# A 31-tap depthwise convolution in a shared PSUM bank: prompt and sample instructions declared independent

## The chip, the cores and the metric

One core of one Trainium2 chip runs the whole program in one launch. The metric is device microseconds (us) of one execution, the median of the runs shown. The engines are named as in the profile: PE is TensorE's matrix multiplication and PEld its weight load, DVE is VectorE, ACT ScalarE, POOL GpSimd, SP SyncE.

## What is computed

One layer of a hybrid decoder for a prompt (16 learned meta tokens and 256 new tokens, 272 columns) and for 8 running sequences with 8 new tokens each (64 columns). A combined input projection feeds a Conformer convolution module and a Mamba-2 (SSD) mixer; an output projection and a layer of product-key experts (PEER) follow. The part that is changed is the depthwise convolution of the Conformer module: each of 1024 channels is filtered along time with 31 taps, over the 30 rows before the new ones (zeros for the prompt, a cache for the sequences) and the new rows.

```python
glu_in, z, xbc, dt_raw, gate_raw = jnp.split(xn @ w_in + b_in, ...)
u = ga * jax.nn.sigmoid(gb)                               # the two halves of glu_in
conf_cat = jnp.concatenate([conf_buf, u], axis=1)         # 30 rows of history, then the new rows
c = causal_depthwise(conf_cat, conf_dw_w, conf_dw_b)      # 31 taps, one filter for each channel
c = jax.nn.silu(layernorm(c, conf_ln_g, conf_ln_b))
y_a = c @ w_conf_out + b_conf_out
...
y = y @ w_m_out                                           # of the SSD mixer
x = x + (g_a * y_a + g_b * y_b) @ w_o
x = x + peer(rmsnorm(x, norm2_w), peer_w_q, peer_keys, peer_u, peer_v)
```

## The kernel before

Features lie on the 128 partitions and tokens in the free dimension: T = 336 columns, first the 64 sample columns (S0 = 64), then the 272 prompt columns (TP). The 1024 channels of the convolution are 8 blocks of 128.

The first stage is a loop over 8 head groups g. For each group it projects four blocks for the SSD mixer (`xbc`, with the short 4-tap convolution `conv_short`, L400 on DVE), two blocks for the gate z (`zproj`), then the two blocks of the Conformer module for the next group (`glu(g+1)`, whose product is written by L459 and L460) and its long convolution (`conf(g+1)` calls `conv_long`), then the decay tables (`decays`), then the SSD step itself (`ssd(g)`). `conf(0)` runs ahead of the loop. After the loop come the layer norm of the convolution's output, the remaining gates, the output projections (to about 620 us) and the expert layer, whose two streams of weights (`eraw`) fill the time from about 700 us to the end.

`conv_long` keeps the running sum of a block in one PSUM tile `pcv` (128 x 336 f32, one bank, one buffer with the tag `pb`). The first tap is a ScalarE activation (L388), the other 30 are `scalar_tensor_tensor` instructions on VectorE (L390): sum = input x tap weight + sum. Each tap is two instructions, one for the 272 prompt columns and one for the 64 sample columns, because the input columns of the sequences are strided. The last tap writes to `cbuf` in SBUF. So a block has 60 instructions on VectorE, and all eight blocks 480.

Within `ssd(g)` VectorE does, among other things: `bst` (L519) and `wsl` (L523), the low parts of split operands; `cbm` (L514), a masked product out of PSUM; `dec` (L516), the decay table times `cbm`; `hs` (L542, L545), the state; `yo` and `xg` (L570, L568), the output; `st` (L584), the new state. TensorE's products `pcb`, `pst`, `pq`, the transposes `ptr` and `pgn` share two PSUM buffers (tag `misc`); `pj` has three.

The order of the instructions on each engine is not written out by hand. The Tile framework draws a dependency between any two instructions that touch the same PSUM bank of a tile when at least one writes, and between those that touch the same data; it plans each engine's order at build time by simulating the program, with the order of the source as priority, and turns each dependency into a semaphore wait. Two VectorE instructions on different columns of `pcv` therefore depend on each other, and each instruction of a block waits for the one before it. The order of ScalarE's table-bound activations is chained by hand (`chain`), and TensorE's order is pinned to the source in the last group (`pin`).

Of the kernel before, what the change touches and what calls it, by code (L numbers as in the profile page):

```python
# [13 lines left out]
OP = mybir.AluOpType  # L14
# [120 lines left out]
def body(tc, ia, oa, stop=None):  # L135
    nc = tc.nc
    with ExitStack() as top:
# [40 lines left out]
        def V(name, j):  # L178
            o, n = VEC[name]
            return vec[:, o + j:o + j + 1]  # L180
# [193 lines left out]
        def samp(ap):  # L374
            return ap.rearrange("p (q c) -> p q c", q=NQ)

        def conv_long(cat, j, dst):
            cs = samp(cat[:, CC + TP:])
            acc = ps.tile([128, T], F32, name="pcv", tag="pb", bufs=1)
            for w in range(CW):  # L380
                wv = V("conf_w", j * CW + w)
                to = dst if w == CW - 1 else acc
                for lo, hi, i_ in ((S0, T, cat[:, w:w + TP]), (0, S0, cs[:, :, w:w + TS])):
                    a_, o = acc[:, lo:hi], to[:, lo:hi]
                    if lo == 0:
                        a_, o = samp(a_), samp(o)
                    if w == 0:
                        nc.scalar.activation(o, i_, AF.Identity, scale=wv, bias=V("conf_b", j))  # L388
                    else:
                        nc.vector.scalar_tensor_tensor(o, i_, wv, a_, op0=OP.mult, op1=OP.add)  # L390

        def conv_short(cat, j, dst, of):
            n = MCAT - MC
# [281 lines left out]
        def conf(g):  # L675
            conv_long(glu(g), g, cb[:, g, :])
            if 0 < g < G - 1:
                nc.gpsimd.tensor_tensor(csum, csum, cb[:, g, :], op=OP.add)
            elif g == 0:
                nc.gpsimd.tensor_copy(csum, cb[:, g, :])  # L680
# [74 lines left out]
        for j in range(KD):  # L755
# [8 lines left out]
                                           op0=OP.mult, op1=OP.subtract)  # L764
# [55 lines left out]
        for k in range(KD):  # L820
            nc.vector.scalar_tensor_tensor(nd[:, k, :], xT[:, k, NGAT:NGAT + ND], V("n2", k), rs2[:, NGAT:NGAT + ND],
                                           op0=OP.mult, op1=OP.mult)
# [521 lines left out]
```

## Time and profile before

| | |
|---|---|
| median of 3 runs | 1453.44 us (1450.84 to 1455.16) |
| the profiled execution | 1455.07 us |
| span in its profile | 1453.3 us, 24685 instructions |
| mean granted TensorE clock | 0.968 |
| busy: PE, DVE, POOL, ACT | 1348.9, 1070.6, 617.2, 527.0 us |

The profiled execution took 1.6 us more than the median; 1.8 us of it lie outside the span. Times in the views count from the span's start. A row of a timeline has the start, the duration, the engine, the source line, the operation, what it writes and reads, the shapes, and a count; neighbours of one kind are merged into one row, whose duration reaches from the first start to the last end, and a row that begins with a prompt instruction (128x272) can hold sample instructions (128x64) too. In brackets stands the idle time of the engine before the row and what ended it. A row of the waits has the total, the number of waits and the longest.

### The profile page before, as it was taken

How to read it: one execution, taken by the hardware profiler on the slowest of the kernel's cores; microseconds unless marked ns; L12 is line 12 of the kernel's file. 1: busy time of each engine (PE TensorE's matmuls, PEld its weight loads, DVE VectorE, ACT ScalarE, POOL GpSimd, SP SyncE). 2: the span in 40 equal slices, each digit the busy share in tenths (PEclk: the TensorE clock that was granted, in tenths of full speed). 3: DMA queues.
4: the chain of work that ended last, by engine and by line, in shares of the span. 5: the costliest groups of instructions: out<-in, count | busy, mean ns of one | idle time of the engine just before them, and what ended most of it. 6: DMA issues, size and time to landing. Idle time of an engine off the chain costs nothing.

```text
span 1453.3 us, 24685 instructions
## 1 busy us (share of the span) xinstructions
PE 1348.9 (93%) x9308; PEld 1276.7 (88%) x9308; DVE 1070.6 (74%) x2343; ACT 527.0 (36%) x1426; POOL 617.2 (42%) x491
## 2 busy tenths in 40 slices
PE   6999988999978999999999988999979999987997
PEld 3888987889857999989899888999979999987997
DVE  6788888888897522568999985877888777776423
ACT  4687657775737443434222221211111101011001
POOL 2267776676755665754221242222332222242200
PEclk9899999999989999999999999999989999999999
DMA  5434434444323344453999899999999999999983
GB/s 196 148 102 164 165 117 136 149 155 161 107 77 102 117 145 145 137 189 102 354 414 413 332 412 415 397 376 391 407 398 415 381 377 371 382 416 416 414 325 95
DMA packets 86807, 382.06 MB, mean 263 GB/s; under 512 B 10112, under 2 KB 15360, under 8 KB 66080
## 3 DMA queue, kind: packets, MB, share of 16 engines
q1 hardware_dynamic: 64144, 226.87, 43.6%
q0 software_dynamic: 20736, 151.00, 25.7%
q10 hardware_dynamic: 1808, 2.61, 0.5%
q8 instruction: 73, 1.20, 0.3%
q14 instruction: 46, 0.38, 0.1%
HBM read 367.41 MB, written 13.03 MB: 262 GB/s over the span
## 4 chain that ended last, share of the span: by engine, by line
PE 66%; DVE 18%; DMA 8%; ACT 6%; issue 1%; POOL 0%; DVEq 0%; ACTq 0%
PE pj L149 25%; PE va L1210 19%; PE pj L1119 11%; PE pg L1148 4%; DMA eraw<-in_vE_dram 3%; DMA eraw<-in_uT_dram 3%; DVE pcv L390 2%; DVE ygat L1053 2%; DVE wuv L1045 2%; PE pst L149 2%; ACT wh L213 1%; ACT dec L194 1%; ACT L194 1%; DVE pj L400 1%; DVE dec L516 1%
## 5 line engine op out<-in xcount | busy, mean ns | idle before, releaser
L933 POOL DMA_INDIRECT wuv<-in_peer_uv_dram,gid x144 | 191.7, 1331 | 503.2 <-DVE ygat L1053 198.5
L214 POOL TENSOR_TENSOR wl<-wraw,wh 128x1024 fp32r<-128x1024 f32 x115 | 278.6, 2424 | 171.0 <-ACT wh L213 77.7
L1119 PE MATMUL pj<-nd,eraw 128*128 128x176 f32 x2048 | 324.2, 318 | 12.2 <-DMA eraw<-in_uT_dram 9.2
L1210 PE MATMUL va<-S,eraw 128*128 128x176 f32 x2048 | 315.4, 314 | 12.2 <-DMA eraw<-in_vE_dram 12.1
L1119 PEld LDWEIGHTS pj<-nd,eraw 128*128 128x128 f32 x2048 | 311.1, 193 | 16.5 <-ACT S L1121 10.0
L1210 PEld LDWEIGHTS va<-S,eraw 128*128 128x128 f32 x2048 | 306.5, 190 | 17.3 <-DMA eraw<-in_vE_dram 15.4
L149 PE MATMUL pj<-ah,wh 128*128 128x336 f32 (+1 forms) x768 | 254.8, 339 | 5.8 <-ACT xg L194 3.6
L149 PE MATMUL pj<-al,wh 128*128 128x336 f32 (+1 forms) x768 | 250.4, 333 | 0.0
L1053 DVE SCALAR_TENSOR_TENSOR ygat<-wuv,scg,ygat 128x1024 f32<-128x1024 f32 x128 | 164.8, 1288 | 54.1 <-ACT scg L1048 51.4
L213 ACT CAST wh<-wraw 128x1024 fp32r<-128x1024 f32 x128 | 135.1, 1056 | 162.3 <-PE pj L149 90.6
L390 DVE SCALAR_TENSOR_TENSOR pcv<-ccat,vec,pcv 128x272 f32<-128x272 f32 x464 | 182.9, 394 | 13.1 <-ACT pcv L388 3.0
L1045 DVE SCALAR_TENSOR_TENSOR wuv<-wuv,x2m 128x1024 f32<-128x1024 f32 x128 | 156.9, 1226 | 38.3 <-DMA wuv<-in_peer_uv_dram,gid 38.3
L1047 ACT ACTIVATE scg<-scg 128x1 f32<-128x1 f32 x144 | 29.1, 202 | 411.1 <-DVE wuv L1045 405.4
L149 PEld LDWEIGHTS pj<-ah,wh 128*128 128x128 f32 x768 | 153.7, 200 | 18.8 <-ACT xg L194 6.2
L149 PEld LDWEIGHTS pj<-al,wh 128*128 128x128 f32 x768 | 153.9, 200 | 1.9 <-issue 0.9
L149 PE MATMUL pj<-ah,wl 128*128 128x336 f32 (+1 forms) x768 | 147.7, 324 | 0.0
L149 PEld LDWEIGHTS pj<-ah,wl 128*128 128x128 f32 x768 | 123.6, 191 | 4.4 <-issue 3.4
L1121 ACT ACTIVATE S<-pj 128x176 f32<-128x176 f32 x128 | 37.6, 311 | 149.1 <-PE pj L1119 146.9
L1148 PE MATMUL pg<-oh 128*128 128x64 bf16 x1056 | 75.1, 241 | 0.0
L1148 PEld LDWEIGHTS <-oh 128*128 128x128 bf16 x1056 | 70.9, 117 | 2.1
L1155 DVE TENSOR_TENSOR S<-S,pg 128x192 f32<-128x192 f32 (+1 forms) x66 | 31.7, 507 | 54.3 <-PE pg L1148 50.0
L400 DVE SCALAR_TENSOR_TENSOR pj<-mcat,vec,pj 128x360 f32<-128x360 f32 x96 | 55.8, 590 | 6.5 <-ACT pj L398 6.3
(355 smaller groups left out, 1814.9 us busy)
## 6 DMA issues: line engine op xcount, KB each, us to landing
eraw<-in_uT_dram SPq DMA_DIRECT2D x128, 512.0 KB
eraw<-in_vE_dram SPq DMA_DIRECT2D x128, 512.0 KB
wraw<-in_w_in_dram SPq DMA_DIRECT2D x80, 512.0 KB
st<-in_state_dram SPq DMA_DIRECT2D x8, 1024.0 KB
out_ssm_s_dram<-st SPq DMA_DIRECT2D x8, 1024.0 KB
wraw<-in_w_mo_dram SPq DMA_DIRECT2D x16, 512.0 KB
wraw<-in_w_q_dram SPq DMA_DIRECT2D x16, 512.0 KB
wraw<-in_w_co_dram SPq DMA_DIRECT2D x8, 512.0 KB
```

The lines of the kernel that those rows point to most:

```text
L149: i_ = nc.tensor.matmul(*a_, **kw)
L213: (nc.vector.tensor_copy if on_dve else nc.scalar.copy)(h, src)
L214: (nc.gpsimd if on_pool else nc.vector).tensor_tensor(l, src, h.bitcast(F32), op=OP.subtract)
L390: nc.vector.scalar_tensor_tensor(o, i_, wv, a_, op0=OP.mult, op1=OP.add)
L400: nc.vector.scalar_tensor_tensor(o, cat[:, w:w + n], wv, o, op0=OP.mult, op1=OP.add)
L933: i_ = nc.gpsimd.indirect_dma_start(out=u, out_offset=None, in_=ia["peer_uv"], in_offset=bass.IndirectOffsetOnAxis(ap=gid[:, c:c + 1], axi ...
L1045: nc.vector.scalar_tensor_tensor(u[:, :D], u[:, :D], 1.0, x2m if c < NPICK else x2e, op0=OP.mult, op1=OP.mult, accum_out=w)
L1053: nc.vector.scalar_tensor_tensor(a_, u[:, D:], scg[:, c:c + 1], a_, op0=OP.mult, op1=OP.add)
L1119: i_ = nc.tensor.matmul(p[:, :ND], raw[:, k, :], nd[:, k, :], start=(k == 0), stop=(k == KD - 1))
L1121: nc.scalar.activation(Sv(b), p[:, :ND], AF.Gelu)
L1148: i_ = nc.tensor.matmul(pg[:, q, :], B[:, q // 4, :, q % 4], A[:, c_, q // 4, :, q % 4], start=(c_ == 0), stop=(c_ == 2))
L1210: i_ = nc.tensor.matmul(va[k // 2][:, k % 2], raw[:, k, :], Sv(b), start=False, stop=(b == 127), skip_group_check=True)
```

## The change

In `conv_long` each VectorE instruction is declared to have no dependency on the VectorE instruction of the same block that was written just before it. Since the two column ranges alternate in the source, that takes away the edges between prompt and sample columns, and leaves those from a tap to the next tap of the same columns. The declaration acts before the order is planned, so it changes the planner's input as well as the waits. No instruction, transfer or buffer changes; the two ScalarE instructions of the first tap keep their edges.

```diff
         def conv_long(cat, j, dst):
             cs = samp(cat[:, CC + TP:])
             acc = ps.tile([128, T], F32, name="pcv", tag="pb", bufs=1)
+            before = None
             for w in range(CW):
                 wv = V("conf_w", j * CW + w)
                 to = dst if w == CW - 1 else acc
...
                     if w == 0:
                         nc.scalar.activation(o, i_, AF.Identity, scale=wv, bias=V("conf_b", j))
                     else:
-                        nc.vector.scalar_tensor_tensor(o, i_, wv, a_, op0=OP.mult, op1=OP.add)
+                        t = nc.vector.scalar_tensor_tensor(o, i_, wv, a_, op0=OP.mult, op1=OP.add)
+                        if before is not None:
+                            tc.declare_no_dep(t.ins, before.ins, reason="prompt and sample columns are disjoint")
+                        before = t
```

## The prediction

> **What bounds the kernel now.** I read the page first: busy shares, then the chain that ended last.
>
> ```profile
> span 1453.3 us, 24685 instructions
> PE 1348.9 (93%) x9308; PEld 1276.7 (88%) x9308; DVE 1070.6 (74%) x2343; ACT 527.0 (36%) x1426; POOL 617.2 (42%) x491
> PE 66%; DVE 18%; DMA 8%; ACT 6%; issue 1%; POOL 0%; DVEq 0%; ACTq 0%
> L390 DVE SCALAR_TENSOR_TENSOR pcv<-ccat,vec,pcv 128x272 f32<-128x272 f32 x464 | 182.9, 394 | 13.1 <-ACT pcv L388 3.0
> ```
>
> TensorE (PE) is busy for 93% of the span and carries two thirds of the chain. The convolution that is changed (L390) is VectorE's (DVE's) largest group of the first stage: 464 instructions here and 16 more that write cbuf, 480 in all. So the question is not what VectorE saves but how much of it TensorE was waiting for. Where the convolution lies, and what each engine does there, is read from the busy times by stage; the columns are the stretch, its length, the busy times of PE, PEld, DVE, ACT and POOL, the granted clock, and DMA:
>
> ```profile
> 143.00:193.00 50.00, 46.92 (x316) 42.11 (x314) 43.52 (x97) 34.01 (x94) 36.15 (x36) 0.97 0.44 146
> 293.00:343.00 50.00, 47.85 (x313) 42.82 (x312) 44.44 (x97) 32.85 (x93) 34.76 (x37) 0.93 0.42 138
> 700.00:1453.00 753.00, 705.74 (x5206) 691.14 (x5204) 555.04 (x1135) 124.94 (x460) 192.00 (x144) 0.98 0.96 378
> ```
>
> All of L390 lies between 50 and 429 us (its first and last rows follow below). There VectorE is near 44 of 50 us busy and TensorE 47 to 48: two nearly full engines, with TensorE losing 2 to 4 us in each head group of 50 us. After 700 us the DMA queues are 96% busy; nothing of the convolution is left there. Then the waits of TensorE from 48 to 440 us (us in total, times, longest):
>
> ```profile
> PE pcb L149 <- DVE cbm L514: 6.3, 4, 2.1
> PE pst L149 <- DVE cbm L514: 5.3, 4, 1.8
> PE pgn L149 <- POOL sq L593: 4.8, 1, 4.8
> PE pq L149 <- DVE hs L545: 3.9, 2, 2.2
> PE pj L149 <- ACT xg L194: 3.6, 6, 1.4
> PE pst L149 <- DVE hs L542: 2.0, 1, 2.0
> ```
>
> VectorE is what TensorE waited for in 6.3 + 5.3 + 3.9 + 2.0 = 17.5 us, in 11 waits, all in the SSD step of a group. This is the pool from which a gain can come. GpSimd's 4.8 us and ScalarE's 3.6 us are not touched.
>
> **The change, part by part.** It adds and removes no instruction and no DMA. It takes away one kind of edge: each L390 instruction loses the edge to the one before it (prompt columns behind sample columns and the reverse). The edge from tap to tap within the same columns stays. Two consequences have to be priced.
>
> First, VectorE's own time. These rows of VectorE's timeline show what the edge costs (start, duration, instruction; a merged row runs from its first start to its last end):
>
> ```profile
> 50.80 3.11 DVE L390 SCALAR_TENSOR_TENSOR pcv<-ccat,vec,pcv 128x272 f32<-128x272 f32 x7 [1.59 <-ACT pcv L388]
> 65.93 6.56 DVE L390 SCALAR_TENSOR_TENSOR pcv<-ccat,vec,pcv 128x272 f32<-128x272 f32 x15
> 107.22 0.28 DVE L390 SCALAR_TENSOR_TENSOR pcv<-ccat,vec,pcv 128x64 f32<-128x64 f32 x1
> 107.41 0.50 DVE L570 TENSOR_TENSOR yo<-po,e 128x336 f32<-128x336 f32 x1
> 108.32 0.50 DVE L390 SCALAR_TENSOR_TENSOR pcv<-ccat,vec,pcv 128x272 f32<-128x272 f32 x1
> 108.73 0.56 DVE L568 SCALAR_TENSOR_TENSOR xg<-xg,vec,py 128x336 f32<-128x336 f32 x1
> 426.17 2.02 DVE L390 SCALAR_TENSOR_TENSOR pcv<-ccat,vec,pcv 128x64 f32<-128x64 f32 x5
> 428.23 0.69 DVE L390 SCALAR_TENSOR_TENSOR cbuf<-ccat,vec,pcv 128x272 f32<-128x272 f32 x2
> ```
>
> When an instruction of other work follows, it starts 0.41 us after a prompt instruction (108.32 to 108.73) and 0.19 us after a sample one, before the 0.50 and 0.28 us are over: two neighbours overlap. The run of 15 is 8 prompt and 7 sample instructions, each waiting for the last: (6.56 - 0.50) / 7 = 0.866 us per pair against 0.41 + 0.19 = 0.60. The edge costs 0.266 us a pair, 0.133 us a neighbour. The edge that stays does not bind: the next tap of the same columns comes 0.60 us later, after the 0.50 us have passed. Over the whole stage the convolution has 73 such unbroken runs (of 50.80 the first; the last is that of 426.17 and 428.23) with 297 neighbours, so VectorE can be freed of 297 x 0.133 = 39.5 us. If those instructions are planned further apart, less is freed; none is the lower end.
>
> The Trainium skill, page "VectorE: DVE Perf Modes", section "The DRAIN you can't avoid", says that the next operation cannot issue until the pipe is empty and that a semaphore between chained operations costs nothing extra. By that rule nothing is freed and the time stays at 1453.4 us. The 0.41 us against a 0.50 us duration speaks against it here; I leave it a small chance.
>
> Second, what of this lies on TensorE's path. I take first that the order stays about as it is. Then a TensorE wait shrinks by 0.133 us for each neighbour that stands in VectorE's queue ahead of the awaited instruction and behind VectorE's last idle time or long operation. For the longest waits:
>
> ```profile
> 136.08 1.68 DVE L390 SCALAR_TENSOR_TENSOR pcv<-ccat,vec,pcv 128x64 f32<-128x64 f32 x4
> 179.10 2.22 DVE L390 SCALAR_TENSOR_TENSOR pcv<-ccat,vec,pcv 128x272 f32<-128x272 f32 x5
> 184.22 1.69 DVE L390 SCALAR_TENSOR_TENSOR pcv<-ccat,vec,pcv 128x272 f32<-128x272 f32 x4
> 186.10 0.49 PE L149 MATMUL pcb<-bc 128*128 128x128 f32 x2 [1.62 <-DVE cbm L514]
> 275.16 2.87 DVE L390 SCALAR_TENSOR_TENSOR pcv<-ccat,vec,pcv 128x64 f32<-128x64 f32 x7
> 279.63 0.49 PE L149 MATMUL pcb<-bc 128*128 128x128 f32 x2 [0.83 <-DVE cbm L514]
> 281.33 1.32 PE L149 MATMUL pst<-wx,xt 16*128 16x256 f32 x4 [1.21 <-DVE cbm L514]
> 318.92 0.82 DVE L390 SCALAR_TENSOR_TENSOR pcv<-ccat,vec,pcv 128x272 f32<-128x272 f32 x2
> 321.18 3.96 DVE L390 SCALAR_TENSOR_TENSOR pcv<-ccat,vec,pcv 128x272 f32<-128x272 f32 x9
> 326.92 0.80 PE L149 MATMUL pcb<-bc 128*128 128x128 f32 x2 [2.06 <-DVE cbm L514]
> 375.35 1.69 DVE L390 SCALAR_TENSOR_TENSOR pcv<-ccat,vec,pcv 128x64 f32<-128x64 f32 x4
> ```
>
> At 326.92 TensorE waited 2.06 us for the cbm product, which stood behind the runs of 318.92 and 321.18, 1 + 8 neighbours: 9 x 0.133 = 1.2 us. By the same count the waits at 279.63 and 281.33 lose 6 x 0.133 = 0.8 us together, the wait at 186.10 loses 7 x 0.133 = 0.9 us, those behind the runs of 136.08 and of 375.35 lose 3 x 0.133 = 0.4 us each, and the two behind hs in these groups 0.1 us each, one neighbour. Sum 3.9 us. The last group's waits (3.5 us of the 17.5) I leave at nothing: a 1.55 us VectorE product and a GpSimd operation stand there.
>
> A wait also costs behind itself. Three rows of the chain, all of the same 336-column matmuls, and the restart after a shorter wait:
>
> ```profile
> 247.02 4.06 PE pj L149 x25
> 282.65 5.24 PE pj L149 x24
> 384.36 5.24 PE pj L149 x24
> 233.41 0.42 PE L149 MATMUL pj<-ah,wh 128*128 128x336 f32 x1 [1.13 <-ACT xg L194]
> 233.97 0.32 PE L149 MATMUL pj<-al,wh 128*128 128x336 f32 x1
> 234.13 0.32 PE L149 MATMUL pj<-ah,wh 128*128 128x336 f32 x1
> ```
>
> At full pace 24 take 24 x 4.06 / 25 = 3.9 us; behind the waits of groups 282 and 384 they take 5.24, so 1.34 us is lost to a lower clock. After the wait of 1.13 us the starts are 0.16 us apart, full pace. The waits at 281 and 326 would fall from 2.04 (0.83 + 1.21) and 2.06 us to 1.2 and 0.9 us, so I count two slow stretches saved: 2.7 us. The ends are none, and all five such stretches, 6.7 us. The Trainium skill, page "TensorE: Matmul & The Clock Gate", section "What's actually happening", puts the slow clock behind an idle window of some 3.4 us. By that none of these waits would slow TensorE and the sum would be 3.9 us; the rows of 5.24 us disagree, since no wait for VectorE in the table is longer than 2.2 us.
>
> Everything else is costed at nothing: ScalarE's first tap and the copies that follow the last one are off TensorE's path, and the queues of SP and GpSimd issue the same DMAs; their cover is TensorE's own 47 us a group. The stages behind 435 us start earlier by what is gained, since the chain runs through TensorE there.
>
> Sum: 3.9 + 2.7 = 6.6 us. The profiled execution took 1455.07 us, 1.6 above the median 1453.44; against its own time the sum gives 1448.5, against the median 1446.8, which is my number. Ends: if every VectorE wait and all slow stretches went, 17.5 + 6.7 = 24.2 us, 1429. If the order turns bad, see the second rival.
>
> **The rivals.** What late comes next: no gain. Behind the cbm product stand ScalarE (xg, six waits) and the doubled-length dec products next to GpSimd work; VectorE's stream is planned ahead of time, and the place that the shorter convolution leaves can be filled with more convolution, so that the awaited instruction starts where it did. For it: VectorE's convolution is always behind, so there is always more to fill in. Against it: it is the same total, and what is done early is missing later. Time: 1453 within 4.4 us (0.3%, about what a measurement of this kernel can tell from no change).
>
> Slower: the convolution crowds out the SSD step. From 181 to 191 us, around the cbm and dec products, seven single convolution instructions stand between other work; the first and the last:
>
> ```profile
> 181.93 0.27 DVE L390 SCALAR_TENSOR_TENSOR pcv<-ccat,vec,pcv 128x64 f32<-128x64 f32 x1
> 189.97 0.28 DVE L390 SCALAR_TENSOR_TENSOR pcv<-ccat,vec,pcv 128x64 f32<-128x64 f32 x1
> ```
>
> They are single because the next one is not ready. Without the edge a pair is ready: each gap then holds 0.60 us in place of 0.30 on average, 7 x 0.30 = 2.1 us more ahead of the cbm and dec products, less the 0.9 us freed: 1.2 us a group, and TensorE already waits there. Seven groups: 8.4 us, and two more slow stretches, 2.7: 1464.5. It decides as soon as more than 0.9 / 0.30 = 3 gaps of a group take a second instruction. For it: the convolution stands earlier in the program than the SSD step of its group. Against it: what the convolution does earlier it no longer does in the next group, and its sum is 39.5 us smaller.
>
> Larger gain: with the two chains free, a group's convolution needs 30 x 0.60 = 18 us in place of the (428.9 - 50.8) / 8 = 47 us that it is spread over now, and could be over before the next SSD step: 1429 to 1438.
>
> **How the numbers follow.** Forecast (6.6 us, its own range 1441 to 1449) 0.42; larger gain 0.05; no gain 0.32, in it 0.04 for the rule that nothing is freed; slower 0.21. Faster by over 0.3% is 0.47, within 0.32, slower 0.21. The low end 1436 leaves most of the larger gain out, the high end 1461 the worse half of the slower case, together some 0.15.
>
> **What the profile after would show.** Right: a run of 15 near 4.7 us (7 x 0.60 + 0.50), TensorE's waits for cbm and hs near 13 us, fewer 24-matmul rows of 5.2 us. Wrong in the first step: the pair still 0.87 us. Wrong in the second: the pair is 0.60 us but the waits for cbm and hs are as long or longer, with pairs of L390 between cbm and dec. It would also be wrong if the plan of another engine changed and a wait on ScalarE or GpSimd took the place.

## The result, and the profile after: 0.8% slower

The changed kernel took 1465.68 us (median of 10 runs, 1457.82 to 1469.35) against 1453.72 us (10 runs, 1450.84 to 1457.41) before: ratio 1.0081, 95% interval 1.0063 to 1.0100. The profiled execution took 1466.60 us. Its page, in the lines that answer to those of before (the source lines behind L379 have moved by 4; the convolution is now L391, cbm L518, dec L520, hs L546 and L549):

```profile
span 1464.8 us, 24692 instructions
PE 1349.3 (92%) x9308; PEld 1276.3 (87%) x9308; DVE 1036.3 (71%) x2343; ACT 526.8 (36%) x1426; POOL 607.9 (42%) x491
PE 65%; DVE 20%; DMA 8%; ACT 5%; issue 2%; POOL 1%; DVEq 0%; ACTq 0%
L391 DVE SCALAR_TENSOR_TENSOR pcv<-ccat,vec,pcv 128x272 f32<-128x272 f32 x464 | 152.8, 386 | 17.4 <-ACT pcv L389 17.4
```

VectorE did get shorter, by 34.3 us (1070.6 to 1036.3), 30.1 of them in the convolution's group (the dec and bst products give 2.9 and 3.2 us more, and other work takes some of that back). It is also less often late: its idle time ahead of the convolution, with ScalarE's first tap as the releaser, is 17.4 us where it was 3.0. The whole loss arises in the first stage. The next two fences hold one row each of the busy times by stretch, from 48 us to the start of the layer norm behind the loop (442 us before, 456 us after); columns as in the prediction, length first, then PE. Before:

```profile
48.00:442.00 394.00, 366.31 (x2402) 324.64 (x2402) 335.69 (x765) 260.52 (x707) 265.63 (x254) 0.95 0.41 137
```

After:

```profile
48.00:456.00 408.00, 371.79 (x2402) 328.27 (x2402) 301.07 (x764) 260.87 (x708) 266.50 (x254) 0.93 0.40 132
```

The same 2402 matmuls take 14 us more: 8.5 us more idle time of TensorE (27.7 to 36.2) and 5.5 us more busy time at a lower granted clock (0.95 to 0.93). From there to the end about 12 us of it are kept. The waits of TensorE in that stretch, after (total, times, longest):

```profile
PE pst L149 <- DVE cbm L518: 8.9, 5, 3.4
PE pcb L149 <- DVE cbm L518: 5.8, 3, 2.3
PE pj L149 <- ACT xg L194: 5.8, 4, 2.3
PE pq L149 <- DVE hs L549: 4.0, 2, 2.4
PE pst L149 <- DVE hs L546: 3.8, 3, 2.8
PE pgn L149 <- POOL sq L597: 3.4, 1, 3.4
PE pj L149 <- DVE pcv L391: 2.8, 2, 2.4
```

For cbm and hs it waits 22.5 us where it was 17.5, and the longest is 3.4 us where it was 2.2. Waits for ScalarE's xg (3.6 before, 5.8 now) and, new, for pcv (2.8) add 5.0 us, and the wait for GpSimd's sq gives 1.4 back. This is how that longest wait looks in the timeline (VectorE, then the waiting TensorE row), and what TensorE does behind a wait of 2.4 us:

```profile
234.29 1.84 DVE L520 TENSOR_TENSOR dec<-dec,cbm 80x320 f32<-80x320 f32 x1
236.06 1.28 DVE L391 SCALAR_TENSOR_TENSOR pcv<-ccat,vec,pcv 128x272 f32<-128x272 f32 x4
237.26 0.58 DVE L404 SCALAR_TENSOR_TENSOR pj<-mcat,vec,pj 128x360 f32<-128x360 f32 x1
237.76 0.68 DVE L391 SCALAR_TENSOR_TENSOR pcv<-ccat,vec,pcv 128x272 f32<-128x272 f32 x2
238.36 0.28 DVE L518 TENSOR_TENSOR cbm<-pcb,cstm 128x128 f32<-128x128 f32 x1
238.69 2.37 PE L149 MATMUL pst<-wx,xt 16*128 16x256 f32 x4 [3.36 <-DVE cbm L518]
...
383.51 0.42 PE L149 MATMUL pj<-ah,wh 128*128 128x336 f32 x1 [2.41 <-DVE pcv L391]
383.77 0.32 PE L149 MATMUL pj<-al,wh 128*128 128x336 f32 x1
...
384.91 0.48 PE L149 MATMUL pj<-ah,wh 128*128 128x336 f32 x1
385.19 0.48 PE L149 MATMUL pj<-al,wh 128*128 128x336 f32 x1
```

Six convolution instructions, in pairs that no longer wait for each other, stand between dec and the cbm product that frees TensorE's PSUM buffer; from start to start they take 1.8 of the 3.36 us (236.06 to 237.26, 237.76 to 238.36). The dec product ahead of them took 1.84 us, where the same product three groups on took 0.47; the last section says what it waited for. Behind the wait that ended at 383.51 the matmuls first start about 0.16 us apart and from 384.9 us on 0.28 us apart: the slow clock comes more than 1 us behind the wait. The clock's own record has it from 384.63 to 388.04 us, as these rows by stretch show (columns as above, the granted clock third from the end):

```profile
381.22:384.63 3.41, 1.12 (x7) 1.12 (x8) 3.41 (x12) 3.23 (x10) 1.62 (x3) 1.00 0.27 64
384.63:388.04 3.41, 3.41 (x15) 3.41 (x14) 3.41 (x8) 2.71 (x8) 2.67 (x1) 0.52 0.22 90
```

### The profile page after: what moved, and what is told of

It reads as the page before. It is cut to its first block, busy times and chain, and to the rows that moved or that the text cites. A ratio compares the mean times of both kernels' runs of the same rounds, so it can differ in the third digit from the quotient of the medians.

```text
span 1464.8 us, 24692 instructions
## 1 busy us (share of the span) xinstructions
PE 1349.3 (92%) x9308; PEld 1276.3 (87%) x9308; DVE 1036.3 (71%) x2343; ACT 526.8 (36%) x1426; POOL 607.9 (42%) x491
## 4 chain that ended last, share of the span: by engine, by line
PE 65%; DVE 20%; DMA 8%; ACT 5%; issue 2%; POOL 1%; DVEq 0%; ACTq 0%
PE pj L149 25%; PE va L1214 19%; PE pj L1123 10%; PE pg L1152 4%; DMA eraw<-in_vE_dram 3%; DVE pcv L391 3%; DVE ygat L1057 2%; DVE wuv L1049 2%; DMA eraw<-in_uT_dram 2%; PE pst L149 2%; DVE pj L404 1%; DVE dec L520 1%; ACT wh L213 1%; ACT L194 1%; PE py L149 1%
## 5 line engine op out<-in xcount | busy, mean ns | idle before, releaser
L937 POOL DMA_INDIRECT wuv<-in_peer_uv_dram,gid x144 | 181.2, 1258 | 512.9 <-DVE ygat L1057 231.9
L391 DVE SCALAR_TENSOR_TENSOR pcv<-ccat,vec,pcv 128x272 f32<-128x272 f32 x464 | 152.8, 386 | 17.4 <-ACT pcv L389 17.4
L1125 ACT ACTIVATE S<-pj 128x176 f32<-128x176 f32 x128 | 37.7, 312 | 152.8 <-PE pj L1123 152.7
```

Source lines behind the costliest of these rows:

```text
L391: t = nc.vector.scalar_tensor_tensor(o, i_, wv, a_, op0=OP.mult, op1=OP.add)
L937: i_ = nc.gpsimd.indirect_dma_start(out=u, out_offset=None, in_=ia["peer_uv"], in_offset=bass.IndirectOffsetOnAxis(ap=gid[:, c:c + 1], axi ...
L1125: nc.scalar.activation(Sv(b), p[:, :ND], AF.Gelu)
```

## The experiments

Each kernel below is the changed one unless it says otherwise. "Held to an order" means that an edge is added from each instruction of an engine to the two ahead of it in a given order; it orders the plan and adds no semaphore wait between instructions of one engine. In the cuts of code `pin_order` stands for the function that adds these edges, and the comments are this text's. Where only some engines are held, the others are planned anew. The ratio is to the kernel before on the same chip, with its 95% interval.

**Waits and order apart.** The change does two things: it takes away waits, and it alters the plan of every engine. Two runs complete the square. The changed kernel on the order of before:

```diff
         body(tc, ia, oa)
+        pin_order(tc, nc)   # all five engines: the order of before
```

> The changed kernel with the instructions of every engine held in the order that the kernel before has; only the waits between prompt and sample columns are gone. Theory A (the new plan is what costs, the freed waits are a gain): faster than before by 2 to 7 us, near 1449, VectorE's busy time some 35 us below 1070.6, TensorE's waits for cbm and hs below 17.5 us. Rival B (the closer spacing itself costs, on the chip, whatever the order): near the changed kernel, 1462 to 1468. Rival C (the waits are neither gain nor loss): 1453.7 within 2 us.

And the kernel before, with all its waits, on the order of the changed one:

```diff
-                        t = nc.vector.scalar_tensor_tensor(...)
-                        if before is not None:
-                            tc.declare_no_dep(t.ins, before.ins, ...)
-                        before = t
+                        nc.vector.scalar_tensor_tensor(...)
...
         body(tc, ia, oa)
+        pin_order(tc, nc)   # all five engines: the order of the changed kernel
```

> The kernel before, with all its waits, and the instructions of every engine held in the order of the changed kernel. Theory A: as slow as the changed kernel or slower, 1466 to 1474, since the new order has the convolution in pairs that now wait again. Rival B: near 1453.7, since the spacing is the old one. Rival C: 1465.7 within 2 us.

| | order of before | new order |
|---|---|---|
| with the waits | 1453.5 us | 1481.66 us, 1.0195 (1.0182 to 1.0208) |
| without | 1451.41 us, 0.9988 (0.9976 to 1.0000) | 1465.68 us, 1.0081 (1.0063 to 1.0100) |

By the ratios, taking the waits away is a gain in both columns (0.12%, 2 us, and 1.14%, 17 us), and the new order is a loss in both rows (1.95%, 28 us, and 0.93%, 14 us). So the loss is the plan's alone. The gain on the old order is at the edge of what was measured: its interval ends at 1.0000, and it fits the expectation of no gain as well as that of a small one. On the new order the waits' share is clear of noise, and the run with them was slower still than the 1474 us expected at most. The stretch to the norm and three of the waits, of the first run, in whose trace TensorE, VectorE, ScalarE and GpSimd all keep the order of before:

```profile
48.00:439.00 391.00, 363.68 (x2402) 322.04 (x2402) 311.74 (x765) 260.74 (x708) 266.33 (x254) 0.96 0.41 138
```

```profile
PE pst L149 <- DVE cbm L518: 5.9, 5, 2.2
PE pj L149 <- ACT xg L194: 5.0, 10, 1.1
PE pcb L149 <- DVE cbm L518: 3.4, 3, 1.8
```

On the old order VectorE's busy time in the stretch falls by 24 us (335.69 to 311.74; some 35 were expected) and TensorE's idle time stays: 27.3 us for 27.7. The cbm waits fall by 2.3 us, the waits for ScalarE's xg rise by 1.4.

**Which engine's order.** Only VectorE is held to the order of before:

```diff
+        pin_order(tc, nc)   # VectorE alone: the order of before
```

> The changed kernel with VectorE's instructions alone held in the order of the kernel before; the other engines are planned anew. If VectorE's order is what costs (A1): 1446 to 1453. If the plan of the other engines costs (A2): above 1458.

1454.30 us, 1.0000 (0.9990 to 1.0011), 1 us above the range expected: 12 of the 14 us are gone, though TensorE, ScalarE and GpSimd were planned anew; TensorE's order came out as neither that of before nor the changed one. The counterpart holds only TensorE to the order of before:

```diff
+        pin_order(tc, nc)   # TensorE alone: the order of before
```

> The changed kernel with TensorE alone held to the order of before and the other engines planned anew. VectorE's new order has the traits of the changed kernel: 291 convolution instructions between bst and the last st of groups 1 to 6 (before 212, changed kernel 281) and two in the gaps of the short convolution. Theory D (what costs is the density of the convolution in the whole SSD step, bst to last st, where VectorE is needed most): 1462-1472. Theory P (what costs is TensorE's new order, which asks for VectorE's products too soon): 1451-1456.

1463.92 us, 1.0077 (1.0064 to 1.0091). Its waits:

```profile
PE pcb L149 <- DVE cbm L518: 10.0, 4, 3.4
PE pst L149 <- DVE cbm L518: 8.8, 5, 3.5
```

With TensorE's old order and a new one on VectorE, the loss is back and sits at cbm: 18.8 us against 11.6 before and 14.7 in the changed kernel. So it is VectorE's order that costs. How ScalarE and GpSimd are planned around it is part of that: their orders were not held apart from it.

**Which part of VectorE's order.** First the planner is told to start the next block's convolution behind the last dec of the group:

```diff
+            for t_ in tap[-2:] if g + 1 < G else ():
+                tc.add_manual_dep(t_, m_.ins.name, <order only>, reason="after dec")
```

> The changed kernel, and the first VectorE taps of a group's convolution are ordered behind the last dec product of the SSD step that they used to meet, so that no convolution stands between bst and dec in groups 1 to 5. Theory A1 (the new plan costs because it puts 18 to 25 convolution instructions ahead of dec instead of 15 to 18): TensorE's waits for cbm and hs fall below 10 us and the time below before, 1440 to 1449. Rival A2 (the new plan costs elsewhere, on TensorE's, ScalarE's or GpSimd's order): the waits for cbm fall but the time stays between 1455 and 1470.

1452.36 us, 0.9994 (0.9980 to 1.0008). The loss is gone, but not for the reason given: TensorE still waits 14.8 + 1.5 us for cbm. In this plan the products themselves are longer, for a reason that the last section gives. The groups of dec, first of the changed kernel:

```profile
L520 DVE TENSOR_TENSOR dec<-dec,cbm 128x512 f32<-128x512 f32 (+1 forms) x24 | 25.9, 1081 | 0.1
```

Then of this run:

```profile
L524 DVE TENSOR_TENSOR dec<-dec,cbm 128x512 f32<-128x512 f32 (+1 forms) x24 | 38.7, 1632 | 0.2
```

The next three, and the four on the gaps behind them, held TensorE, GpSimd and SyncE and moved instructions in VectorE's order by hand; ScalarE was planned anew. Group 3, where c is a convolution instruction, s one of the short convolution, B, W, M, D the products bst, wsl, cbm, dec, and o others, hs among them:

```diff
-BccWccccccccMccDccccsccMsMccDsoD
+BWMDsMsMDsoDcccccccccccccccccccc
```

> The changed kernel with TensorE, GpSimd and SyncE held to its own order and VectorE's too, but with the convolution instructions that stand between a group's bst and its last dec (8, 13, 24, 20, 18, 23, 25, 0 in groups 0 to 7) put right behind that last dec. Theory A (too many convolution instructions in these windows are what costs): TensorE's waits for cbm and hs fall from 22.5 us to under 12 and the time to 1446-1454. Theory B (the windows are not the place: what costs is how the rest of VectorE's stream or the other engines were placed): 1460-1467, the waits turn up at xg or the norm. Theory C (the windows are long anyway since dec and bst wait for others): waits for cbm stay near 15 us, 1452-1458.

1491.35 us, 1.0257 (1.0239 to 1.0276): much slower, and none of the three expectations held.

```profile
PE pq L149 <- DVE hs L549: 19.5, 6, 9.1
PE pj L149 <- ACT xg L194: 16.9, 7, 6.3
PE pst L149 <- DVE hs L546: 8.5, 2, 7.7
...
PE pcb L149 <- DVE cbm L518: 2.8, 2, 1.5
```

The waits for cbm did go, from 14.7 to 5.3 us (the last row and 2.5 us of pst). What was cleared stands in a lump ahead of hs and of the short convolution instead, and TensorE waits there, up to 9.1 us. With 12 instructions left in each window:

> As the run above, but the first 12 convolution instructions of each window stay (8 in group 0, 0 in group 7) and only what is above 12 goes behind the last dec: 55 instructions of the groups 1 to 6 move instead of 131. Theory A, with the dose counting: 12 is fewer than the 14 to 18 of the order before, so 1448-1455, and a few us above the cleared one. If a threshold matters and not the dose, the same as the cleared one. Theory B: 1460-1467.

1468.27 us, 1.0101 (1.0083 to 1.0119): cbm 9.7 us, hs 13.7, xg 8.5; again no expectation held. The wait moves with the instructions. The same clearing of the old order:

> The changed kernel held to the order of before (as in the run of that order that took 1451.4 us), with the convolution of the windows (17, 15, 18, 15, 14, 16, 17, 7) put behind the last dec. Theory A: the 9.3 us that TensorE still waits for cbm fall to 3 or less and the time to 1440-1447. Theory C (without the convolution the window is as long, since dec and bst run beside GpSimd and wait for TensorE): 1449-1453. A third possibility: the convolution is then late and its last block delays the norm: up to 1456.

1473.65 us, 1.0139 (1.0120 to 1.0158). An order that was good is spoiled by it, again through hs. So the number of convolution instructions between bst and dec does not set the time by itself; but these three cannot say where they would cost nothing.

**The gaps of the short convolution.** In the order of before, 53 of 64 gaps between the taps of the short convolution hold one convolution instruction, and 3 hold two; in the changed kernel 62 hold two. So each chain of three taps gets longer.

```diff
-sccsccscc   (changed)
+scscscccc   (e8)      ssscccccc   (e9)
-scscscc     (order of before)
+sccsccs     (e10)     ssscccc     (e11)
```

> In the order of before, one convolution instruction stands in nearly every gap between the three VectorE taps of the short convolution (67 instructions in 62 gaps), in the changed kernel exactly two stand in every gap (a prompt and sample pair, 124 between the same taps and 137 with those that a neighbouring chain shares). Here the changed kernel's own order is held on TensorE, GpSimd, SyncE and VectorE, but in each gap only one stays and the other goes right behind the third tap (65 instructions move, none of the windows from bst to dec is emptied otherwise). Theory S (the doubled gaps in the short convolution's chain are what costs): the chains, from first tap to last, get 65 x 0.30 = 20 us shorter in sum and the time falls to 1450-1459. Theory T (it is what stands ahead of cbm, dec and hs, and the short chains are hidden): within 4 us of 1465.7.

> As the run above with no convolution instruction left in any gap of the short convolution (137 move behind the third taps). Theory S: 1444-1456, below the run with single gaps unless the lumps of four behind the third tap delay what comes next, which would give the same as single gaps. Theory T: 1462-1470.

> The changed kernel held to the order of before, but gaps of the short convolution that hold one convolution instruction take a second, the next in line (41 instructions pulled forward; nothing else moves; the rest would cross the end of a block). Theory S: 41 x 0.30 = 12 us more in the short chains, of which the larger part reaches TensorE: 1457-1466 against the 1451.4 of the order of before. Theory T: within 3 us of 1451.4.

> The changed kernel held to the order of before, with all 67 convolution instructions in the gaps of the short convolution put behind the third tap. Theory S: 1440-1449, the best of all. Theory T: 1450-1455.

Measured 1465.00 (1.0076, 1.0060 to 1.0092), 1462.57 (1.0070, 1.0054 to 1.0086), 1454.89 (1.0010, 1.0000 to 1.0021) and 1448.39 us (0.9980, 0.9967 to 0.9993). Against the ratio of the order on which each is built (1.0081 or 0.9988), the gaps are worth some 3 us: doubled +0.22%, 3.2 us; emptied -0.11% and -0.08%, 1.6 and 1.2 us, less than the intervals tell apart; made single in the new order, -0.05%. Most of the 14 us is not there. The last of the four has the lowest median of the study, and it lies in the range that was expected if the gaps were what costs; but it is 0.2% below the kernel before and only 0.1% below its own order with the gaps filled.

**Spreading it by hand.** The convolution between bst and the last new state (st) of a group, 281 instructions in groups 1 to 6 where before had 212, was thinned to 36 and to 42 a group:

```diff
-BccWcc...  39, 47, 48, 45, 49, 53 convolution instructions up to the last st
+BccWc...   36 (or 42) each, the surplus three by three behind the items after it
```

> The changed kernel with VectorE held to its new order, but the convolution between bst and the last st of a group thinned evenly to 36 instructions (it was 39, 47, 48, 45, 49, 53 in groups 1 to 6), the surplus right behind the last st; the other engines are planned anew. 216 in groups 1 to 6, near the 212 of before. Theory D: 1450-1456. If it is not the density but where single lumps stand: 1460-1468.

> As the run above, thinned to 42 (249 in groups 1 to 6, half way between the order of before and the changed kernel). Theory D with the cost in proportion: half way, 1457-1462.

1478.03 us (1.0165, 1.0150 to 1.0179) and 1472.21 us (1.0122, 1.0104 to 1.0140). The surplus landed between the two glu products and ahead of the next group's transposes, and TensorE waited there instead (4.4 us for one product ahead of pcb, 3.6 for the transposes' copies, both in the first of the two). This says nothing on the density, only that a hand's move makes a new lump.

**Part of the change, with the planner at work.** Half of the blocks each, and one of the two edges:

```diff
-                        if before is not None:
+                        if before is not None and j < 4:       # e15
+                        if before is not None and j >= 4:      # e16
+                        if before is not None and lo == 0:     # e17: only prompt to sample of one tap
```

> The declaration only for the blocks 0 to 3 of the convolution (computed up to head group 2); the blocks 4 to 7 keep their waits and everything is planned anew. Up to the fourth group the changed kernel was not behind the one before (+0.6 us at the fourth glu), so if the loss is made group by group where the free pairs stand (theory G): 1450-1455. If the new plan is bad from the start and only shows later (theory L): 1459-1466.

> The declaration only for the blocks 4 to 7 (groups 3 to 6). Theory G: the groups 3 to 6 make the whole loss, 1461-1467. Theory L: 1452-1457.

> Only the edge from the prompt instruction to the sample instruction of the same tap is taken away; the sample instruction's edge to the next tap's prompt instruction stays. A pair then takes 0.408 + 0.325 = 0.73 us instead of 0.87 (0.60 in the changed kernel). The plan has 244 convolution instructions from bst to the last st of groups 1 to 6 (before 212, changed 281) and 108 from bst to the last dec of groups 1 to 6 (before 95, changed 123). If the cost grows with how many are planned there: 1456-1461, between the two. If any new plan costs the same: 1463-1468. If the waits that stay keep the plan as it was: 1450-1454.

1457.77 us (1.0030, 1.0019 to 1.0041), 1457.22 us (1.0017, 1.0003 to 1.0031) and 1451.51 us (0.9983, 0.9974 to 0.9992). The halves cost 0.30% and 0.17% where the whole costs 0.81%, in neither case what an expectation said. The third is the surprise: it has two instructions in the same 62 gaps as the changed kernel, 108 convolution instructions between bst and dec in groups 1 to 6 (before 95, changed 123), and is a little faster than before. The time fits the third expectation, but not for its reason, since the plan did change. Its stretch to the norm, and its waits (the row behind the dots is of the stretch behind the norm):

```profile
48.00:445.00 397.00, 368.73 (x2402) 327.21 (x2402) 310.20 (x764) 261.43 (x709) 266.09 (x254) 0.94 0.40 136
```

```profile
PE pst L149 <- DVE cbm L518: 17.6, 7, 4.3
PE pcb L149 <- DVE cbm L518: 4.0, 3, 2.3
PE pj L149 <- ACT xnf L194: 2.1, 1, 2.1
...
PE pgb L149 <- DVE xg L619: 2.0, 2, 1.0
```

It waits longer for cbm than the changed kernel (21.6 us against 14.7), but 3.9 us for hs where that waits 7.8, and not for xg (5.8), so that TensorE's idle time is 28.3 us, near the 27.7 of before. It reaches the norm 3 us later than before and makes 2.6 us good behind it, where TensorE's wait for xg was longer in the kernel before:

```profile
PE pgb L149 <- DVE xg L615: 4.6, 2, 3.6
```

So no single count in VectorE's order goes with the time: neither the gaps, nor the instructions between bst and dec, nor cbm's waits alone. Nearest to it comes TensorE's idle time up to the norm: 27.3, 28.3, 28.3 and 30.4 us in the runs at 1451 to 1454 us (old order, whole pairs, start behind dec, VectorE's old order), 36.2 and 36.7 at 1465.7 and 1463.9 (changed, TensorE's old order), 46.1 at 1481.7 and 58.4 at 1491.4. It is not all: the new order without gaps idled for 32.6 us only and took 1462.6; there TensorE's busy time was 370.4 us, at a lower clock, where the old order had 363.7.

## Why the prediction was wrong

**VectorE's own time: right.** A pair takes 0.60 us (start to start 0.408 behind a prompt instruction and 0.192 behind a sample one; before, 0.542 and 0.325), so the 0.133 us a neighbour were right, and on the order of before, which has the same 297 neighbours, the 39.5 us. The convolution's busy time shows less of it, 28.2 us there and 30.1 in the changed kernel, because some 0.04 us of each neighbour's 0.133 was a gap between two instructions. The Trainium skill, page "VectorE: DVE Perf Modes", section "The DRAIN you can't avoid", as the prediction read it, would have freed nothing; these rows disagree with that. The same section adds that a next operation that is not held starts earlier, and with that they agree.

**The step that failed** is "I take first that the order stays about as it is". The declaration acts before the plan is made, as the section on the change says, and a rival was built on it; the sum was nevertheless worked out on the old order, and a worse one was given 0.21. The first experiment is the case that I priced: a gain of about 2 us, which is within no change. The new order costs 14 us on top, by VectorE's part of it.

**The terms, on the order for which they were worked out.** 3.9 us of waits and 2.7 us of slow stretches were forecast, 6.6 in sum; so the term of the waits was too large even there. The run of that order gained 1.7 us (ratio 0.9988; 0 to 3.5 us). By its profile TensorE's busy time fell by 2.6 us, the size of the second term, but its idle time only by 0.4. VectorE's waits for cbm and hs fell from 17.5 to 15.5, and xg took 1.4 of that back: the rival "what late comes next", in small.

**The rival that hit** (slower, 1464.5 us) had the number and the sign, and its first part was literally there: gaps that held one instruction hold two, in the short convolution's chain, part of which runs between the cbm and dec products, and from bst to the last dec stand 123 convolution instructions in groups 1 to 6 where 95 stood. Its price is not borne out, so the near hit is in part luck. It put 8.4 us on waits around cbm and dec; the waits for cbm and hs grew by 5.0. And the plan of whole pairs, with all 62 doubled gaps, 108 instructions in these windows and longer waits for cbm, took 1451.5 us. Emptying the windows by hand cost time; with the planner at work it took the loss away, but left the waits for cbm. Its reason, that the convolution stands earlier in the source, was not tested.

**The slow clock: right in kind.** The Trainium skill, page "TensorE: Matmul & The Clock Gate", section "What's actually happening", puts it behind an idle window of some 3.4 us. Here the rows at 383.51 to 385.19 show it behind a wait of 2.41 us: the 3.41 us ahead of the slow stretch were not idle, TensorE was busy for 1.12 of them. TensorE's busy time, longer at the lower clock, made 5.5 of the 14 us.

**What stays open** is which trait of VectorE's new order costs. That its order carries the loss, with what ScalarE and GpSimd do around it, is shown from two sides (VectorE's put back, TensorE's put back); that it costs through TensorE's waits and the clock is read from the profiles. Six runs that moved instructions by hand within that order settle only that some 3 us at most, by the medians, lie in the gaps of the short convolution, and that these instructions in a lump ahead of hs cost more than spread ahead of cbm.

## What to carry to other kernels

An edge that is taken away is an input to the planner before it is a wait saved: price the two apart, and measure them apart by holding the order, since here taking the waits away was worth -2 us on the old order and the new plan +14. Where two engines are nearly full, a large saving on the one that is not the bound (30 us of VectorE's convolution) is worth only what the other waited for, and a new order can move those waits by more: TensorE's idle time up to the norm went from 27 to 58 us over the orders run here. If the new plan is worse, try part of the declaration: freeing only the pair within a tap kept 22 of the 30 us (the convolution's busy time was 160.8 us, for 182.9 before and 152.8) and cost nothing.

## What the hardware showed that I had not expected

The 24 dec products took 25.9 us in the changed kernel and 38.7 us when the convolution between them was moved away (mean 1.08 and 1.63 us, the same instructions on the same data). The eight bst products went from 7.0 to 15.7 us. Their length depends on where they stand in the plan, so that a stretch that is emptied need not shrink by what was taken out. The traces show what lengthens them: a GpSimd product that is already running. Two rows of each engine, of the run with the convolution behind dec (the last merges a long dec product and a short one):

```profile
327.93 2.35 POOL L214 TENSOR_TENSOR wl<-wraw,wh 128x1024 fp32r<-128x1024 f32 x1 [0.87 <-POOL wx L514]
328.02 2.60 DVE L524 TENSOR_TENSOR dec<-dec,cbm 80x320 f32<-80x320 f32 x1
331.31 2.35 POOL L214 TENSOR_TENSOR wl<-wraw,wh 128x1024 fp32r<-128x1024 f32 x1
331.45 3.36 DVE L524 TENSOR_TENSOR dec<-dec,cbm 128x512 f32<-128x512 f32 x2
```

Every dec product over 1.2 us, 8 in the changed kernel and 12 in this run, started while GpSimd's wl was running, and ended 0.34 us (80x320) or 0.55 us (128x512) behind the end of it; those that started with GpSimd idle took 0.47 to 0.48 and 0.67 to 0.69 us. The longest wait of the section on the result holds such a case: its dec product of 234.29 us started behind a wl that ran from 233.41 to 235.79. This is not the changed kernel's loss, since its dec and bst products are shorter in sum than before (28.8 and 10.2 us), and the run with the longest ones was no slower than before.

And the slow clock does not begin at a wait: behind one of 2.41 us TensorE ran at full pace for more than 1 us before its starts went from 0.16 to 0.28 us apart. In the clock's record of the changed kernel every slow stretch but the one that the end cuts off is a whole multiple of 3.41 us long, and they start whole multiples of 3.41 us apart; so how long behind a wait the slow clock comes seems to depend on where the wait falls in this raster.
